# Keys one step ahead, row norms in groups, the second tile's load on another queue, cached latents loaded sooner

## The chip, the cores and the metric

The kernel runs on one core of a Trainium2 chip. The metric is device time in microseconds (us) of one execution; of a set of runs the median counts. In the profile TensorE is PE (matmuls) and PEld (its weight loads), VectorE is DVE, ScalarE is ACT, GpSimd is POOL and SyncE, which issues the transfers, is SP. Each engine works through its own queue in order and waits on semaphores for what other engines and transfers make.

## What is computed

Two layers of a streaming encoder with three kinds of heads side by side, for 1024 prompt frames (8 tiles of 128) and 32 sample frames (a ninth tile), 1024 wide. A layer is, cut to what matters here:

```python
h = _rmsnorm(x, norm_g)                      # x * rsqrt(mean(x*x) + EPS) * g
z = h @ w_in                                 # retention | latent attention | chunk band
ret_o = retention(...)                       # 4 heads, decayed state
cq, ckv_new, kr_new = ...                    # low-rank queries, latent keys and values, shared rope key
ckv_all = concat(past ckv, ckv_new)          # the sample's 128 cached latents come first
kv = ckv_all @ mla_w_ukv;  q = cq @ mla_w_uq # 8 heads, keys of 64 + 32
mla_o = softmax(q k / sqrt(96)) v            # chunk-causal in the prompt, dense in the sample
band_o = softmax(q k / 8 + bias) v           # the last 8 chunks of 64
y = x + concat(ret_o * silu(g_a), mla_o * silu(g_b), band_o * silu(g_c)) @ w_out
```

All of it is float32; matrix products are made of a high and a low part of each operand.

## The kernel before

**Stages.** For each layer `layer_in` (line 1447) multiplies the nine tiles by eleven column blocks of `w_in`, in the order of STEPS (line 42): b (the latents) first, then blocks for retention and the band, and four blocks of gates. `chunk` (line 525) does a block for eight of them: for each of the nine tiles eight row groups of three matmuls into a bank of tag pj (two banks), then a callback that unloads the bank. `mla` (line 823) then walks over 64 units (head pair, block of 128 queries, head) of scores, transposes and values, while the output product `out_part` (line 1398) is put between the units.

**The order of the work.** Everything beside the main loops is a generator in a list of tasks (`spawn`, line 253). After each step of a main loop `poll` (line 298) advances those tasks that are ready by a hand-made clock (a task is ready again 450 ns after its last step unless GAPS says otherwise), that don't exceed the number allowed for their kind (STREAMS: three prep tasks, two b tasks, one mla task at a time) and that have pages: all tiles in SBUF come from 60 pages of 512 columns (`page`, `free`), and `safe` (line 256) keeps enough of them for the tasks that have started. That is the program's order. The framework then orders each engine's instructions by a timeline model of its own (line 1660), with the program's order as priority; tasks of kind mla have a raised one (line 51).

**The opening.** For the first layer the tiles come transposed from memory. `first_prep` (line 482) is a task per tile: it loads two halves xt, all on SP; splits them into high and low parts in the arena H; squares and sums them (ScalarE, GpSimd, and a reduction xsq on VectorE); has a matmul with ones sum over the partitions, copies that sum (st, line 503) and makes the row's norm r from it on GpSimd (`rstd`). The rows' norms are applied after the projection: as a scale where a bank is unloaded (`unload`, line 551, for which r is enough), and in the gates, where rows lie along the columns, by a product with rb. For that the task spreads r over 128 columns (rrep, line 509), transposes it on TensorE and copies it into rb. `run` (line 1542) starts the opening by hand:

```python
self.step_task(self.fg[0])      # loads of tile 0
self.fetch(0, "b", E0)          # eight weight tiles of block b
self.step_task(self.fg[0])      # parts of tile 0
self.step_task(self.fg[1])      # loads of tile 1
self.poll()
```

When tile 2 of block b is done, `load_bias` (line 393) builds the band's bias: rows are copied to memory (bt), read back with a step (braw), and made into bT on VectorE.

**The sample's cached latents.** `cache_task` (line 611) takes the 128 cached latents through the same products as a tile: it loads cc (two transfers), transposes it on TensorE at once, and goes on with `kv_task`. It is spawned at the ninth tile of block b and runs when two b tasks or fewer are before it.

**The keys.** `mla_pair` (line 786) turns the keys and queries of two heads into transposed high and low parts in H. It has four turns (keys and queries, two halves each); a turn's two loads (sk or sq, from the buffers kd and qd in memory) are issued in the step of the turn before, but those of the first turn in the same step as its transposes. The first pair of a layer is a task that starts in the last gate block and has to be finished before the units begin; the other three are advanced by `mla` one step per unit, from the third of the 16 units of a head pair on.

Of the kernel before, what the change touches and what calls it, by code (L numbers as in the profile page):

```python
# [13 lines left out]
OP = mybir.AluOpType  # L14
# [6 lines left out]
NS = 32  # L21
# [77 lines left out]
class Kern:  # L99
# [382 lines left out]
    def first_prep(self, t, hT):  # L482

        A = self.A
        n = 128 if t < 8 else NS
        xt = [self.page([4, n], name="xt") for _ in range(2)]
        for j in range(2):
            self.load(xt[j], (A["xt_p"][t] if t < 8 else A["xt_s"])[:, 4 * j:4 * j + 4])
        yield
        for j in range(2):  # L490
            self.parts(t, j, xt[j], hT, LO0[j])
        yield
        for x in xt:
            self.act(x, x, AF.Square, scale=1.0 / 32)
        self.tt(xt[0], xt[0], xt[1], OP.add, eng="G")
        sq = self.page([n], name="xsq")
        self.red(sq, xt[0].rearrange("p k n -> p n k"))
        self.free(*xt)
        yield
        p = self.bank((1,), "prep")  # L500
        self.mm(p[:n], sq, self.ones, True, True)
        s1 = self.st(1)
        self.nc.vector.tensor_copy(s1[:n], p[:n])
        r = self.rstd(s1, n, 1, self.r0[:, t:t + 1])
        self.free(sq)
        self.prepped.add(t)
        yield
        rep = self.page([128], name="rrep")
        self.ts(rep[:n], r[:n].to_broadcast([n, 128]), 1.0, None, OP.mult)
        p = self.bank((n,), "prep")  # L510
        self.tr(p, rep[:n])
        self.free(rep)
        self.act(self.rb[t // 4][:, 128 * (t % 4):128 * (t % 4) + n], p)
        yield

    def new_hT(self):
        self.prepped = set()
# [92 lines left out]

    def cache_task(self, l):
        A = self.A
        c = self.page([160], name="cc")
        self.load(c[:, :128], A["c_ckv"][l, 0])
        self.load(c[:, 128:160], A["c_kr"][l, 0])
        p = self.bank((128,), "b")
        self.tr(p, c[:, :128])
        ch, cl = self.page([3, 128], F32R, name="cch"), self.page([3, 128], F32R, name="ccl")
        self.hilo(p, ch[:, 2], cl[:, 2])
        yield  # L620
        yield from self.kv_task(l, 9, 128, ch, cl, c[:, 128:160])
        self.free(c, ch, cl)
        self.b_done()
# [162 lines left out]
    def mla_pair(self, l, hp):  # L786

        turns = [(name, half) for name in ("k", "q") for half in range(2)]
        src = dict(k=self.kd[l], q=self.qd[l])

        def stage(name, half):
            r = []
            for b in (2 * half, 2 * half + 1):
                t = self.page([2, 192], name="s" + name)
                self.load(t, src[name][hp, 256 * b:256 * b + 256, :].rearrange("(a p) e -> p a e", p=128))
                r.append(t)
            return r

        nxt = stage(*turns[0])
        self.vals[hp] = []  # L800
        for n, (name, half) in enumerate(turns):
            cur = nxt
            if n < 3:
                nxt = stage(*turns[n + 1])
            j, col = (0, 1) if name == "k" else (2, 0)
            for i in range(2):
                hs = self.sets[(2 * hp + i) % 4]
                p = self.bank((4, 128), "mprep")
                for b in range(4):
                    self.tr(p[:96, b], cur[b // 2][:, b % 2, 96 * i:96 * i + 96])  # L810
                pf = p[:96].rearrange("p a b -> p (a b)")
                sl = slice(512 * half, 512 * half + 512)
                self.hilo_g(pf, self.cols[:96, col:col + 1], hs[:96, j, sl], hs[:96, j + 1, sl])
                if i:
                    self.free(*cur)
                if n == 3 and not i:
                    for b in range(2):
                        t = self.page([4, 128], name="sv")
                        self.load(t, self.vd[l][hp, 512 * b:512 * b + 512, :].rearrange("(a p) e -> p a e", p=128))
                        self.vals[hp].append(t)  # L820
                yield
# [625 lines left out]
    def layer_in(self, l, hT):  # L1447
        A = self.A
        w = A["w_in"][l]
        self.qs, self.ks, self.vs = [None] * 2, [[None] * 2 for _ in range(2)], [None] * 2  # L1450
        self.mix, self.mixed = {}, set()
        self.bks = None
        self.spare = False
        self.turns, self.full, self.bfull, self.scored = 0, 0, 0, False
        self.bk, self.bv, self.bqt, self.bvp, self.buse = {}, {}, {}, {}, {}
        self.bleft = NB + 2
        self.bq, self.bkdone = set(), set()
        zk = {}

        def cb_b(t, p):  # L1460
            self.spawn("b", self.b_task(l, t, self.unload(t, p, 416)), lambda: "u" in self.W)
            if t == MISC_T:
                self.spawn("misc", self.misc_task(l))
            if t == 8:
                self.spawn("b", self.cache_task(l), lambda: "u" in self.W)
                self.spawn("smp", self.mla_sample(l), lambda: not self.bleft)

        def cb_ak(t, p):
            zk[t] = self.page([512], name="zk")
            self.unload(t, p, 256, z=zk[t][:, :256])  # L1470

        def cb_av(t, p):
            self.unload(t, p, 256, z=zk[t][:, 256:])

        def cb_aq(t, p):
            if t == 0:
                self.ret_state(l)
            self.spawn("ret", self.ret_task(l, t, zk.pop(t), self.unload(t, p, 256)))

        def cb_ck(t, p):  # L1480
            self.spawn("bk", self.band_k_task(l, t, self.unload(t, p, 256)))

        def cb_cv(t, p):
            self.band_v(l, t, p)

        def cb_cq(t, p):
            self.spawn("bq", self.band_task(l, t, self.unload(t, p, 256)))
            if t < 8 and t % 2 == 1:
                pr = t // 2
                self.spawn("band", self.band_attn(l, pr), lambda: all(  # L1490
                    x in self.bq and x in self.bkdone for x in (2 * pr, 2 * pr + 1)) and (not pr or pr - 1 in self.buse))

        fts = dict(ag=(0, 1), bg0=(2, 3), bg1=(4, 5), cg=(6, 7))
        cbs = dict(b=cb_b, ak=cb_ak, av=cb_av, aq=cb_aq, ck=cb_ck, cv=cb_cv, cq=cb_cq)

        def gen(name):
            if name in fts:
                return self.gates(self.W.pop(name), fts[name], hT, name == STEPS[-1])
            return self.chunk(self.W.pop(name), 416 if name == "b" else 256, hT, cbs[name])

        self.spawn("mla", self.mla_pair(l, 0), lambda: self.turns >= 4 and not self.bleft)
        for name, nxt in zip(STEPS, STEPS[1:] + (None,)):
            todo = ([("u", AHEAD_U)] if name == "b" else []) + ([(nxt, AHEAD)] if nxt else [])
            if name not in self.W:
                self.press(lambda: not self.safe(NEED_W[name]))
                self.fetch(l, name)
            n = 0
            for _ in gen(name):
                n += 1
                if todo and n >= todo[0][1] and self.safe(NEED_W.get(todo[0][0], 9)):  # L1510
                    self.fetch(l, todo.pop(0)[0])
                self.poll()
                self.press(lambda: len(self.fg) > CAP or not self.safe(2))
            for x, _ in todo:
                self.press(lambda: not self.safe(NEED_W.get(x, 9)))
                self.fetch(l, x)
# [25 lines left out]
    def run(self):  # L1542
        A = self.A
# [7 lines left out]
        rows = lambda y: (lambda t: y[128 * t:min(T, 128 * t + 128)])  # L1551
        for t in range(9):
            self.spawn("prep", self.first_prep(t, hT))
        self.step_task(self.fg[0])
        self.fetch(0, "b", E0)
        self.step_task(self.fg[0])
        self.step_task(self.fg[1])
        self.poll()
        self.load(self.tab, A["tab"])
        self.load_layer(0)  # L1560
# [1 line left out]
        for l in range(DEPTH):  # L1562
# [22 lines left out]
            bulk, need, n = [None, None], [0, 0], 0.0  # L1585
# [10 lines left out]
            for x, _ in enumerate(self.mla(l)):  # L1596
# [5 lines left out]
                n = min(n + RATES[2 if ended[0] else x % 16 >= SMALL], 2.0)  # L1602
                while n >= 1:
                    i = int(ended[0])
# [62 lines left out]
```

## Time and profile before

| | |
|---|---|
| median of 3 runs | 1388.73 us (1382.41, 1388.73, 1390.26) |
| the profiled execution | 1391.21 us |
| its span, first to last instruction | 1389.4 us |
| mean granted clock of TensorE | 0.992 |
| instructions | 28577 |
| ScalarE, VectorE, GpSimd busy | 760.1, 849.3, 463.7 us |
| transfers | 130.56 MB, 94 GB/s over the span |

The profile is of one execution, with times from the start of its span. A wait names the engine and line that waited, then what it waited for. A line in the code can be that of a helper (177 is every matmul, 183 every transpose, 187 every ScalarE operation), so tiles tell more than lines. PEclk is the share of full clock that TensorE was granted: 1.00 is 2.4 GHz and 0.50 is 1.2 GHz.

### The profile page before, as it was taken

The numbers are of one execution on the slowest core, as the hardware profiler recorded it, in microseconds if no ns is written. First come the engines' busy times: TensorE is split into PE (matmuls) and PEld (weight loads), VectorE is DVE, ScalarE is ACT, GpSimd is POOL, SyncE is SP. The second block draws the span as 40 slices with busy tenths as digits, with TensorE's granted clock in tenths as the row PEclk, the third lists the DMA queues.
The fourth block names the chain that finished last, engine by engine and source line by source line (L and its number), as shares of the span: only waits on it lengthen the run. The fifth ranks groups of instructions, "written<-read, shape, count | busy, mean of one in ns | idle before, by whom it ended". The sixth has DMA issues, their size and how long they took to land.

```text
span 1389.4 us, 28577 instructions
## 1 busy us (share of the span) xinstructions
PE 1327.5 (96%) x10339; PEld 1213.8 (87%) x10339; DVE 849.3 (61%) x2564; ACT 760.1 (55%) x2186; POOL 463.7 (33%) x686
## 2 busy tenths in 40 slices
PE   6899999999998899999999999999999999999998
PEld 6899989999898788877889999989989988888787
DVE  7655657666766656665562555655766765666543
ACT  6545545353655756676672445454555665766551
POOL 4655767343000312221123456755420012312110
PEclk9999999999999999999999999999999999999999
DMA  7334341131211433522340344221212123433131
GB/s 237 106 91 148 116 115 39 39 92 36 64 51 34 145 109 109 159 72 89 107 154 12 110 130 136 82 68 32 85 43 76 47 81 118 148 111 115 61 127 65
DMA packets 131077, 130.56 MB, mean 94 GB/s; under 512 B 14392, under 2 KB 107256, under 8 KB 130936
## 3 DMA queue, kind: packets, MB, share of 16 engines
q1 hardware_dynamic: 130936, 128.74, 30.0%
q8 instruction: 81, 1.33, 0.4%
q14 instruction: 60, 0.49, 0.1%
HBM read 84.48 MB, written 45.79 MB: 94 GB/s over the span
## 4 chain that ended last, share of the span: by engine, by line
PE 76%; DMA 9%; DVE 5%; ACT 4%; POOL 2%; issue 2%; SPq 1%; ACTq 0%; DVEq 0%; POOLq 0%
PE pj L177 46%; PE ps L177 10%; PE s L177 10%; PE ps L183 7%; DMA raw<-in_w_in 3%; PE pj L183 2%; DMA sk<-kd 2%; POOL rs L242 2%; DMA raw<-in_w_out 1%; PE s L183 1%; SPq L247 1%; DMA braw<-bt 1%; ACT whi L187 1%; DVE st L214 1%; ACT PT L187 1%
## 5 line engine op out<-in xcount | busy, mean ns | idle before, releaser
L177 PE MATMUL pj<-whi,H 128*128 128x256 f32 (+1 forms) x1792 | 368.1, 297 | 12.8 <-DVE whi L203 7.1
L177 PEld LDWEIGHTS pj<-whi,H 128*128 128x128 f32 x1792 | 295.1, 192 | 16.8 <-ACT xt L187 7.0
L177 PE MATMUL pj<-wlo,H 128*128 128x256 f32 (+1 forms) x896 | 264.8, 296 | 1.3 <-DVE wlo L210 1.3
L177 PE MATMUL pj<-H,whi 128*128 128x256 f32 (+1 forms) x1024 | 205.6, 293 | 4.0 <-DVE th L210 1.6
L195 POOL TENSOR_TENSOR mlo<-mix,mhi 128x256 fp32r<-128x256 f32 x96 | 70.1, 750 | 378.7 <-ACT mhi L187 179.0
L187 ACT ACTIVATE PT<-ps 128x384 f32<-128x384 f32 (+3 forms) x304 | 130.9, 456 | 113.4 <-PE ps L183 112.4
L177 PEld LDWEIGHTS pj<-wlo,H 128*128 128x128 f32 x896 | 171.9, 192 | 3.6 <-DVE wlo L210 2.2
L177 PEld LDWEIGHTS pj<-H,whi 128*128 128x128 f32 x1024 | 163.0, 191 | 7.3 <-DVE th L210 2.0
L242 POOL TENSOR_TENSOR rs<-ms,nhalf 128x4 f32<-128x4 f32 (+5 forms) x141 | 165.1, 1171 | 9.2
L177 PE MATMUL pj<-H,wlo 128*128 128x256 f32 (+1 forms) x512 | 149.2, 291 | 0.3 <-DVE wlo L210 0.3
L203 POOL TENSOR_SCALAR ms<-st 128x4 f32<-128x4 f32 (+6 forms) x166 | 59.3, 357 | 229.3 <-DVE st L214 194.6
L177 PE MATMUL s<-H 96*128 96x384 f32 (+3 forms) x516 | 128.9, 364 | 3.1 <-ACT P L187 2.9
L187 ACT ACTIVATE whi<-raw,cols 128x256 fp32r<-128x256 f32 (+2 forms) x178 | 83.2, 516 | 75.8 <-DMA raw<-in_w_in 59.7
L214 DVE TENSOR_REDUCE st<-s 128x1 f32<-128x384 f32 (+3 forms) x220 | 118.3, 538 | 8.9 <-PE s L177 6.6
L210 DVE SCALAR_TENSOR_TENSOR wlo<-raw,cols,whi 128x256 fp32r<-128x256 f32 (+2 forms) x184 | 90.7, 525 | 47.7 <-ACT whi L187 47.0
L187 ACT ACTIVATE P<-s,st 128x384 f32<-128x384 f32 (+3 forms) x172 | 99.9, 588 | 22.3 <-DVE st L203 21.9
L177 PE MATMUL pj<-whi,mhi 128*128 128x512 f32 x256 | 103.2, 403 | 3.5 <-DVE st L203 2.2
L177 PE MATMUL pj<-wlo,mhi 128*128 128x512 f32 x256 | 100.7, 393 | 0.0
L177 PE MATMUL pj<-whi,mlo 128*128 128x512 f32 x256 | 100.5, 396 | 0.1
L177 PEld LDWEIGHTS pj<-H,wlo 128*128 128x128 f32 x512 | 98.0, 191 | 1.4 <-DVE wlo L210 0.9
L195 POOL TENSOR_TENSOR wlo<-raw,whi 128x512 fp32r<-128x512 f32 x32 | 40.7, 1285 | 169.5 <-PE s L177 113.5
L177 PEld LDWEIGHTS s<-H 96*128 96x128 f32 x516 | 84.0, 189 | 12.8 <-ACT P L187 6.1
(262 smaller groups left out, 2816.0 us busy)
## 6 DMA issues: line engine op xcount, KB each, us to landing
raw<-in_w_in SPq DMA_DIRECT2D x80, 256.0 KB, 3.1
raw<-in_w_out SPq DMA_DIRECT2D x32, 256.0 KB, 2.9
yp<-yres SPq DMA_DIRECT2D x32, 256.0 KB, 2.0
yres<-yp SPq DMA_DIRECT2D x32, 256.0 KB, 2.8
qd<-qn SPq DMA_DIRECT2D x32, 192.0 KB, 1.9
kd<-kt SPq DMA_DIRECT2D x32, 192.0 KB, 2.0
sk<-kd SPq DMA_DIRECT2D x32, 192.0 KB, 3.6
sq<-qd SPq DMA_DIRECT2D x32, 192.0 KB, 2.6
```

The lines of the kernel that those rows point to most:

```text
L177: self.nc.tensor.matmul(out, lhsT, rhs, start=start, stop=stop)
L183: self.nc.tensor.transpose(out, in_, self.ident[:k, :k])
L187: r = self.nc.scalar.activation(out, in_, func, **kw)
L195: (self.nc.vector if eng == "D" else self.nc.gpsimd).tensor_tensor(out, a, b, op=op)
L203: (self.nc.vector if eng == "D" else self.nc.gpsimd).tensor_scalar(out, a, s1, s2, op0=op0, **kw)
L210: self.nc.vector.scalar_tensor_tensor(out, a, s, b, op0=op0, op1=op1)
L214: self.nc.vector.tensor_reduce(out, in_, axis=AX.X, op=op, negate=negate)
L242: self.nc.gpsimd.tensor_tensor(r[:n], ms[:n], self.nhalf[:n, :w], op=OP.pow)
L247: self.nc.sync.dma_start(dst, src)
```

## The change

Four edits. A `yield` in `mla_pair` makes a step of its own of the first turn's loads. `first_prep` ends at the norm r, and a new task `row_norms` spreads the norms of four tiles at a time into rb; it is spawned at the ninth tile of block b in the first layer. The second tile's loads are issued by ScalarE and stand, with tile 0's, ahead of the fetch of the weights. The cached latents are loaded in the callback of the eighth tile of block b (t == 7), into a page that is held until `cache_task` ends.

```diff
@@ -485,7 +485,8 @@
         n = 128 if t < 8 else NS
         xt = [self.page([4, n], name="xt") for _ in range(2)]
         for j in range(2):
-            self.load(xt[j], (A["xt_p"][t] if t < 8 else A["xt_s"])[:, 4 * j:4 * j + 4])
+            (self.nc.scalar if t == 1 else self.nc.sync).dma_start(
+                xt[j], (A["xt_p"][t] if t < 8 else A["xt_s"])[:, 4 * j:4 * j + 4])
         yield
         for j in range(2):
             self.parts(t, j, xt[j], hT, LO0[j])
@@ -501,17 +502,24 @@
         self.mm(p[:n], sq, self.ones, True, True)
         s1 = self.st(1)
         self.nc.vector.tensor_copy(s1[:n], p[:n])
-        r = self.rstd(s1, n, 1, self.r0[:, t:t + 1])
+        self.rstd(s1, n, 1, self.r0[:, t:t + 1])
         self.free(sq)
         self.prepped.add(t)
         yield
-        rep = self.page([128], name="rrep")
-        self.ts(rep[:n], r[:n].to_broadcast([n, 128]), 1.0, None, OP.mult)
-        p = self.bank((n,), "prep")
-        self.tr(p, rep[:n])
-        self.free(rep)
-        self.act(self.rb[t // 4][:, 128 * (t % 4):128 * (t % 4) + n], p)
-        yield
+
+    def row_norms(self):
+
+        for g, n in enumerate((128, 128, NS)):
+            m = 4 if g < 2 else 1
+            rep = self.page([m, 128], name="rrep")
+            self.ts(rep[:n], self.r0[:n, 4 * g:4 * g + m].unsqueeze(2).to_broadcast([n, m, 128]), 1.0, None, OP.mult)
+            yield
+            p = self.bank((m, n), "prep")
+            for i in range(m):
+                self.tr(p[:, i], rep[:n, i])
+            self.free(rep)
+            self.act(self.rb[g], p.rearrange("p a b -> p (a b)"))
+            yield
 
     def new_hT(self):
         self.prepped = set()
@@ -610,9 +618,7 @@
 
     def cache_task(self, l):
         A = self.A
-        c = self.page([160], name="cc")
-        self.load(c[:, :128], A["c_ckv"][l, 0])
-        self.load(c[:, 128:160], A["c_kr"][l, 0])
+        c = self.cc
         p = self.bank((128,), "b")
         self.tr(p, c[:, :128])
         ch, cl = self.page([3, 128], F32R, name="cch"), self.page([3, 128], F32R, name="ccl")
@@ -797,6 +803,7 @@
             return r
 
         nxt = stage(*turns[0])
+        yield
         self.vals[hp] = []
         for n, (name, half) in enumerate(turns):
             cur = nxt
@@ -1461,7 +1468,13 @@
             self.spawn("b", self.b_task(l, t, self.unload(t, p, 416)), lambda: "u" in self.W)
             if t == MISC_T:
                 self.spawn("misc", self.misc_task(l))
+            if t == 7:
+                self.cc = self.page([160], name="cc")
+                self.load(self.cc[:, :128], A["c_ckv"][l, 0])
+                self.load(self.cc[:, 128:160], A["c_kr"][l, 0])
             if t == 8:
+                if self.rb is not None:
+                    self.spawn("prep", self.row_norms())
                 self.spawn("b", self.cache_task(l), lambda: "u" in self.W)
                 self.spawn("smp", self.mla_sample(l), lambda: not self.bleft)
 
@@ -1551,10 +1564,12 @@
         rows = lambda y: (lambda t: y[128 * t:min(T, 128 * t + 128)])
         for t in range(9):
             self.spawn("prep", self.first_prep(t, hT))
-        self.step_task(self.fg[0])
+        first, second = self.fg[:2]
+        self.step_task(first)
+        self.step_task(second)
         self.fetch(0, "b", E0)
-        self.step_task(self.fg[0])
-        self.step_task(self.fg[1])
+        self.step_task(first)
+        self.step_task(second)
         self.poll()
         self.load(self.tab, A["tab"])
         self.load_layer(0)
```

## Rows read from the trace of the kernel before

**Rows 1.** The page, part 1: busy us (share of the span) and instructions

```profile
PE 1327.5 (96%) x10339; PEld 1213.8 (87%) x10339; DVE 849.3 (61%) x2564; ACT 760.1 (55%) x2186; POOL 463.7 (33%) x686
```

**Rows 2.** PE's waits, whole span: line, releaser, us in total, times, longest

```profile
PE pj L183 <- DMA sk<-kd: 4.9, 5, 1.2
PE s L183 <- DVE rrep L203: 4.7, 1, 4.7
...
PE s L177 <- DVE xsq L214: 2.3, 1, 2.3
...
PE ps L183 <- DMA cc<-in_c_ckv: 2.2, 1, 2.2
```

**Rows 3.** Stretches of the opening: us, engines' busy us, PEclk, DMA share, GB/s

```profile
7.00:15.50 8.50, 7.17 (x19) 5.99 (x20) 8.50 (x15) 4.42 (x7) 1.30 (x1) 1.00 1.01 361
...
38.50:43.30 4.80, 0.07 (x2) 0.03 (x2) 1.37 (x5) 1.26 (x7) 1.17 (x3) 0.96 0.58 177
43.30:50.00 6.70, 6.70 (x22) 6.45 (x23) 5.28 (x18) 5.49 (x13) 5.12 (x11) 0.52 0.51 153
```

**Rows 4.** DVE's timeline, 41 to 46 us: start, us, instruction [idle before]

```profile
41.66 0.62 DVE L203 TENSOR_SCALAR bT<-braw 128x256 f32<-128x256 f32 x2 [4.17 <-DMA braw<-bt]
...
43.00 0.22 DVE L203 TENSOR_SCALAR rrep<-r 128x128 f32<-128x128 f32 x1
...
44.99 0.14 DVE L503 COPY st<-s 128x1 f32<-128x1 f32 x1
```

**Rows 5.** POOL's and ACT's timelines, 47 to 49 us

```profile
47.80 0.80 POOL L242 TENSOR_TENSOR r<-ms,nhalf 128x1 f32<-128x1 f32 x1
...
48.63 0.61 ACT L187 ACTIVATE z<-pj,r 128x416 f32<-128x416 f32 x1
```

**Rows 6.** Chain of waits, 0 to 80 us: start us, us, what

```profile
24.30 4.63 PE pj L177 x24
...
44.40 7.10 PE pj L177 x24
```

**Rows 7.** Tiles rrep and rb: operation, count, min/median/max ns, first and last start us

```profile
L203 DVE TENSOR_SCALAR rrep<-r x9: 213/227/1312, 19.9 to 67.2; 128x128 f32<-128x128 f32 x8, 32x128 f32<-32x128 f32 x1
...
L187 ACT ACTIVATE rb<-s x9: 228/269/297, 24.0 to 70.0; 128x128 f32<-128x128 f32 x8, 128x32 f32<-128x32 f32 x1
...
L195 DVE TENSOR_TENSOR u<-pj,rb x40: 180/424/426, 243.0 to 441.9; 128x256 f32<-128x256 f32 x32, 128x32 f32<-128x32 f32 x8
```

**Rows 8.** SP's and POOL's timelines at the opening

```profile
2.58 3.75 SPq L247 DMA_DIRECT2D raw<-in_w_in  x8
6.48 2.07 SPq L247 DMA_DIRECT2D xt<-in_xt_p  x4
...
19.85 2.52 POOL L195 TENSOR_TENSOR xt<-xt,xt 128x512 f32<-128x512 f32 x2
```

**Rows 9.** Transfers, whole span: count, KB each, median us to landing

```profile
xt<-in_xt_p SPq DMA_DIRECT2D x16, 256.0 KB, 4.9
```

**Rows 10.** PE's timeline, 410 to 415 and at 915 us

```profile
410.02 0.42 PE L183 MATMUL pj<-ident,sk 128*96 128x128 f32 x2 [1.14 <-DMA sk<-kd]
...
414.67 0.60 PE L183 MATMUL pj<-ident,sk 128*96 128x128 f32 x4
...
915.20 0.33 PE L183 MATMUL ps<-ident,cc 128*128 128x128 f32 x1 [2.15 <-DMA cc<-in_c_ckv]
```

**Rows 11.** Stretches at the band attention and the cached latents (columns as rows 3)

```profile
421.80:428.60 6.80, 6.39 (x48) 5.74 (x49) 2.02 (x10) 1.16 (x4) 0.00 (x0) 0.50 0.44 130
428.60:470.00 41.40, 36.28 (x344) 33.21 (x344) 27.57 (x110) 27.84 (x88) 5.88 (x6) 1.00 0.22 65
...
916.70:920.10 3.40, 3.40 (x16) 3.27 (x16) 2.10 (x8) 2.49 (x7) 2.00 (x2) 0.50 0.00 0
```

**Rows 12.** Chain of waits, whole span: two steps 16 units apart

```profile
511.85 3.97 DMA sk<-kd
...
566.56 4.00 DMA sk<-kd
```

## The prediction

> **What bounds the kernel now.** I read four views in this order. First the page's busy times: TensorE (PE) is busy for 1327.5 of 1389.4 us [rows 1], so the other engines cost time only where they make PE stop, and all its stops together are 1389.4 - 1327.5 = 61.9 us. Second, the waits of PE: four of the things it waits for are touched by the change [rows 2], the loads of the keys (sk, 4.9 us in 5 stops), the spread row norm (rrep, 4.7 us in one), the squared sums (xsq, 2.3 us in one) and the sample's cached latents (cc, 2.2 us in one). That is 14.1 us, a fifth of the idle time. Third, the stretches with PE's granted clock, because a stop is followed by slow work: after the rrep stop PE is busy throughout 43.3 to 50 us, at a clock of 0.52 [rows 3], and 1.5 us after the cc stop it runs 3.4 us at 0.50 [rows 11]. Fourth, the timelines at each stop, to see what the missing input itself waited for.
>
> The sum is made against the profiled execution (1391.2 us, span 1389.4). It stands 2.5 us above the median of the three runs, 1388.7, so a total found on it is taken off the median.
>
> **Part 1, row norms in groups.** The nine rrep copies on VectorE (DVE), of about 0.23 us, and nine evacuations into rb on ScalarE, of about 0.27 us [rows 7], become three and three; the nine transposes on PE stay. All move from the opening to after the last tile of the first projection. They are first read at 243 us [rows 7], some 170 us later, so the moved work lies beside PE's projection work and I cost it at nothing; without that cover three groups would stop PE for at most a DVE operation each, about 1 us in all.
> What counts is where the old rrep stood. At 38.5 us PE meets a transpose of rrep. DVE can't make it: its queue stands before bT, which waits 4.17 us for the band bias's rows (braw), and rrep comes behind bT, at 43.00 [rows 4]. So PE does nothing from 38.5 to 43.3 (0.07 us busy of 4.80) [rows 3]. The 24 matmuls of the next tile were ready, and then run at the half clock: 7.10 us, against 4.63 us for 24 at full clock [rows 6]. The stop costs 4.73 and the clock 2.47, together 7.2 us.
> Not all of it comes back. DVE still waits for braw. Behind bT stands also the copy st at 44.99 [rows 4], from which GpSimd makes the norm r at 47.80, which ScalarE needs for the unload z at 48.63 [rows 5]; only that frees one of the two banks of tag pj, which the tile after next needs. PE would then work on its ready tile from 38.5 to about 43.2 and stop again until 48.63 + 0.61 = 49.2, where before it began that later tile at about 52.1: 2.9 us gained. That is the low end; 7.2 is the high end, if the copy st now comes ahead of bT, as its matmul, no longer behind the transpose, runs 5 us earlier. I take 5.0, the middle.
>
> **Part 2, the second tile's load on ScalarE.** Two loads of 256 KB [rows 9] leave ScalarE's queue ahead of the eight weight loads, where SyncE (SP) had issued them at 6.48, behind those (2.58 to 6.33) [rows 8]. Issuing costs ScalarE nothing: it has no tile to work on before the first one has landed. The gain is the xsq stop of 2.3 us [rows 2]: GpSimd's sum for that tile came at 19.85 [rows 8], and an earlier tile lets it come earlier. The price: the transfer engines are full here (share 1.01 at 361 GB/s) [rows 3], so 512 KB put ahead of the weights delay them by up to 512 KB / 361 GB/s = 1.45 us, and the first matmul with them. The lower bound is 0: a weight tile serves three matmuls, at half clock 7.10 / 8 = 0.9 us [rows 6], so the weights behind the first have time. I take the middle, 0.7. Net -1.6 us, between +1.45 and -2.3.
> A rule of the Trainium skill speaks against this part: "Trainium Kernel Development and Optimization", section Key Constraints, says that loads issued from several engines' queues all run on the same 16 transfer engines and interleave, so that another queue saves only time of issue. By it the sum would take the whole 1.45 us, leave part 2 at -0.85 and end at 1380. No load leaves another queue than SP's in this trace, so it doesn't show this.
>
> **Part 3, the cached latents.** In each layer two small loads move from the start of the cache task (912 us in layer 1) to the eighth tile of the first projection, over 100 us earlier; on SP that is the same issues in another place, behind nothing but their page. Layer 0 doesn't stop PE for them. In layer 1 the transpose waits 2.15 us [rows 10], and the half clock from 916.7 takes half of 3.40 us, 1.7 [rows 11]. High end 3.9; low end 0, if PE then waits for something else. I take 3.0, the whole stop and half of the clock. The cost is one page of 60 held through the layer's projections. With 59 left I put it at nothing; were a fetch of weights to wait for it, PE would stop about as it does here, for 2.2 to 3.9 us a time.
>
> **Part 4, the keys a step ahead.** The first two loads of a head pair are issued one step before their transposes: per layer four pairs, the same 32 loads in all. In the attention stage a step is one unit, (566.56 - 511.85) / 16 = 3.4 us [rows 12], while the loads of a step take 4.0 us [rows 12] and the five stops are about 1 us each, 1.2 at most [rows 2], the one at 410.02 among them [rows 10]. A load 3.4 us earlier covers each of them. High end 4.9 us, all of [rows 2]'s sk line; low end 0. I take 3.5, since behind some stops PE next waits for a DVE result of the scores. The pair's work then ends one step later of sixteen, which its readers, a whole head pair further on, don't see; the first pair of a layer is the exception (third rival).
>
> **Sum:** 5.0 + 1.6 + 3.0 + 3.5 = 13.1 us. Program order changes on every queue from the first microseconds on, so small stops elsewhere (48 of the 61.9 us are not touched) are drawn anew; I take off 3 us, as a removed stop seldom leaves all later ones as they were. That leaves 10: 1388.7 - 10 = **1379 us**.
>
> **The rivals.** (a) The DVE queue decides the opening: it still stands 4.17 us at bT, and the stop only moves from the transpose to the pj bank. For it: the st to z chain [rows 4, 5]. Against: the copy's matmul is ready 5 us sooner. Then part 1 gives 2.9 less a new half-clock stretch of 2.5, so 0.4; total 0.4 + 1.6 + 3.0 + 3.5 - 3 = 5.5, or 1383 us, no change that can be told.
> (b) The change doesn't do what it says on the queues: the issue order is made by a scheduler from a timeline model, and a load that is earlier in the program may stay where it was. For it: nothing forces SP to issue sk before the step; against: the loads so far left when their step came, or PE would not have had to wait for them. Part 4 gives nothing, and the total is 10 - 3.5 = 6.5, or 1382 us, just within.
> (c) Slower: the first pair's extra step. Each layer starts its attention only once that pair is done, in a stretch in which PE has little else: from 428.6 to 470 it is busy for 36.28 of 41.40 us, and from 421.8 to 428.6 at clock 0.50 [rows 11]. The first two steps of the pair lie 414.67 - 410.02 = 4.65 us apart [rows 10]. A step more costs up to 4.65 plus a half-clock stretch of 3.4 in each of two layers, 16.1 us, and is felt where the projections' work ends before the pair does. If also part 1 gives only its 0.4, the total is 16.1 - 0.4 - 1.6 - 3.0 - 3.5 + 3 = +10.6, or 1399 us. Against it: the extra step adds no work, and the scores of the chunk band stand beside it.
>
> **How the numbers follow.** A measurement can tell about 0.5%, 6.9 us, from no change: faster is below 1381.8, slower above 1395.6. Forecast 0.51 and, with all terms at their high ends, 0.06, both faster; (a) 0.18 and (b) 0.15, both within; (c) 0.10, slower. So faster 0.57, same 0.33, slower 0.10. The low end of the range takes all high ends, 7.2 + 2.3 + 3.9 + 4.9 = 18.3, and half the spread of the three runs, 4 us: 1366. The high end takes (a) with (b), 1388.7 - 2, and the same 4 us with a little of (c): 1392. The cases of "faster" alone hold 1366 to 1382.
>
> **What would show it.** In the changed profile: no rrep row among PE's waits and no long PE stop at 38.5; the stretch that held 43.3 to 50 at clock 0.9 or more; no cc and no sk in PE's waits; the second tile's loads on ScalarE's queue within 3 us, and the first matmul at 7.1 to 8.5; PE idle of 50 to 54 us in all instead of 61.9. I am wrong in part 1 if PE stops 4 us or more between 38 and 50 us for H or for a pj bank; in part 4 if sk waits stay; in the whole if PE's idle time outside the four lines grows by more than 5 us, in the stretch of (c) above all.

## The result and the profile after

The changed kernel takes 1409.12 us, median of 4 runs (1407.32 to 1410.15), beside 1387.3 us for the kernel before on the same chip (4 runs): 1.0161 times as long, 95% interval 1.0141 to 1.0181. I had forecast 1379, and 1366 to 1392 as the range; it is 22 us slower. The profiled execution took 1410.15 us, its span is 1407.6 us, its mean granted clock 0.984.

First the busy times of the changed kernel, from part 1 of the profile's page, to be read against [rows 1]:

```profile
span 1407.6 us, 28566 instructions
...
PE 1340.1 (95%) x10339; PEld 1220.5 (87%) x10339; DVE 846.5 (60%) x2556; ACT 762.0 (54%) x2178; POOL 458.1 (33%) x686
```

The same 10339 matmuls keep PE busy for 12.6 us more, and PE's stops come to 1407.6 - 1340.1 = 67.5 us, 5.6 more. Next PE's waits in the changed kernel (line, releaser, us in total, times, longest), the counterpart of [rows 2]:

```profile
PE pj L177 <- DVE whi L203: 8.1, 1, 8.1
PE pj L177 <- ACT zk L187: 7.8, 3, 3.2
PE s L177 <- ACT P L187: 5.9, 7, 1.7
PE ps L183 <- ACT P L187: 4.6, 8, 1.4
PE s L177 <- DVE xsq L214: 3.9, 1, 3.9
...
PE pj L183 <- DMA sk<-kd: 0.7, 2, 0.5
```

The four lines that the change aimed at fell from 14.1 us to 4.6: no rrep and no cc are left, sk fell from 4.9 to 0.7, and xsq rose from 2.3 to 3.9. Other waits grew by more than that: the first matmul begins at 8.1 us instead of 7.1, and a bank of tag pj that ScalarE unloads into zk is waited for 7.8 us instead of 3.7.

The longer busy time is half-clock time. These are the stretches between the opening's start and the last microseconds at which the granted clock was at its lower level (1.2 GHz), first of the kernel before, then of the changed one (us, busy us and count of each engine, PEclk, DMA share, GB/s; the last line sums them):

```profile
42.90:49.70 6.80, 6.42 (x21) 6.18 (x22) 5.61 (x20) 5.49 (x13) 4.82 (x10) 0.50 0.56 169
...
sum 20.40, PE 19.62 PEld 18.49 DVE 12.55 ACT 11.21 POOL 6.82; mean PE 4.90 PEld 4.62 DVE 3.14 ACT 2.80 POOL 1.71
```

```profile
110.90:114.30 3.40, 3.40 (x18) 3.40 (x17) 1.58 (x4) 1.43 (x8) 1.93 (x3) 0.50 0.54 175
...
1029.10:1039.30 10.20, 10.20 (x48) 7.88 (x48) 4.42 (x16) 4.31 (x14) 1.25 (x2) 0.50 0.13 32
...
sum 44.20, PE 41.70 PEld 36.93 DVE 24.82 ACT 26.97 POOL 16.33; mean PE 5.21 PEld 4.62 DVE 3.10 ACT 3.37 POOL 2.04
```

Four stretches have become eight. In the changed kernel's opening one 128x416 matmul follows another after 0.35 us in the half-clock stretch from 26 us on, and after 0.19 us at 15 to 16 us, at full clock. Full clock would thus have saved about 45% of PE's time in such stretches: by that estimate 0.45 x (41.7 - 19.6) = 10 of the 12.6 us come from there. So beside the kernel before, the loss is small stops, spread over both layers, and half-clock work behind some of them. Where the old rrep stop was, the clock did get better, though not to the 0.9 that I had named: 43.3 to 50 us now has 0.75 instead of 0.52 [rows 3]. The stretch at 916.7 to 920.1, behind the old cc stop, has 1.00 instead of 0.50 [rows 11].

### The profile page after: what moved, and what is told of

Same layout as the page of the kernel before. It is cut to its first block, busy times and chain, and to the rows that moved or that the text cites. A ratio compares the mean times of both kernels' runs of the same rounds, so it can differ in the third digit from the quotient of the medians.

```text
span 1407.6 us, 28566 instructions
## 1 busy us (share of the span) xinstructions
PE 1340.1 (95%) x10339; PEld 1220.5 (87%) x10339; DVE 846.5 (60%) x2556; ACT 762.0 (54%) x2178; POOL 458.1 (33%) x686
## 5 line engine op out<-in xcount | busy, mean ns | idle before, releaser
L177 PE MATMUL pj<-H,whi 128*128 128x256 f32 (+1 forms) x1024 | 209.4, 295 | 4.6 <-DVE th L210 2.6
L242 POOL TENSOR_TENSOR rs<-ms,nhalf 128x4 f32<-128x4 f32 (+4 forms) x141 | 166.1, 1178 | 9.5
L203 POOL TENSOR_SCALAR ms<-st 128x4 f32<-128x4 f32 (+5 forms) x166 | 55.5, 334 | 241.1 <-DVE st L214 194.8
```

The costliest lines, as they stand in the source:

```text
L177: self.nc.tensor.matmul(out, lhsT, rhs, start=start, stop=stop)
L203: (self.nc.vector if eng == "D" else self.nc.gpsimd).tensor_scalar(out, a, s1, s2, op0=op0, **kw)
L242: self.nc.gpsimd.tensor_tensor(r[:n], ms[:n], self.nhalf[:n, :w], op=OP.pow)
```

## The experiments

Theories: **(P)** the page that part 3 holds from the eighth tile of block b until the cache task ends is short elsewhere, and what goes without it comes late; **(R)** any edit draws the order of all queues anew, and this draw came out badly; **(T)** part 3's transfers themselves, or part 2's, collide with weights. All ratios are to the kernel before, run on the same chip beside it. Letters name the parts: r row norms, a second tile, c cached latents, y keys a step ahead.

**Each part alone,** put into the kernel before; the full lines stand in the diff above. s1 (a):

```diff
-            self.load(xt[j], ...)
+            (self.nc.scalar if t == 1 else self.nc.sync).dma_start(xt[j], ...)
@@ run
-        self.step_task(self.fg[0])
+        first, second = self.fg[:2]
+        self.step_task(first)
+        self.step_task(second)
         self.fetch(0, "b", E0)
...
```

s2 (r) takes the spread out of `first_prep`, s3 (c) loads and holds early, s4 (y) adds the step:

```diff
+                if self.rb is not None:                      # s2, at t == 8
+                    self.spawn("prep", self.row_norms())
```

```diff
+            if t == 7:                                       # s3
+                self.cc = self.page([160], name="cc")
+                self.load(self.cc[:, :128], A["c_ckv"][l, 0])
+                self.load(self.cc[:, 128:160], A["c_kr"][l, 0])
```

```diff
         nxt = stage(*turns[0])
+        yield                                                # s4
```

> The kernel before with one of the four edits: the second tile's loads issued by ScalarE ahead of the weights. Three theories of where the +22 us come from. Spread: every edit redraws the order of work, the loss is many small stops in places that no edit touches, and the four single edits give between -6 and +8 us each and don't add up to +22. Held page: the cached latents' page, held from the eighth tile on, is nearly all of the loss; this edit without it gives -4 to +2 us, 1383 to 1389. Pair's step: the extra step of a head pair makes the loss; here again -4 to +2. The changed kernel's own opening (the first matmul 1.1 us later, the stop for xsq 3.9 us instead of 2.3) should be seen here if it is this edit's: a first matmul at 8.1 us.

> The kernel before with the row norms spread in groups after the first projection, and nothing else. My forecast of its part: the stop of 4.7 us for rrep goes, -3 to -7 us, 1380 to 1384. Spread: -6 to +8 us. Held page and pair's step: -5 to 0, since neither is here. If the 9 us that the changed kernel loses between 75 and 120 us come from the spreading now being done there, this kernel loses them too and stands at 1390 or more.

> The kernel before with the cached latents loaded at the eighth tile into a page that is held until their task, and nothing else. Held page: +10 to +22 us, 1397 to 1409, with waits of ScalarE for stores (a page that is written again before its store has landed) and PE stops behind them between 70 and 400 us in layer 0. Spread: -6 to +8. Pair's step: -4 to 0, as the cc stop of 2.2 us goes.

> The kernel before with the first pair of key loads in a step of its own, and nothing else. Pair's step: +9 to +22 us, most of it in layer 1's attention (1040 to 1340 us in the changed kernel, which loses 14 us there). Held page: -5 to 0, the sk stops of 4.9 us gone. Spread: -6 to +8 us.

Measured: a 1.0052 (1.0033 to 1.0070), +7 us; r 0.9967 (0.9945 to 0.9989), -4.6 us by the ratio, -2.9 by the medians; c 1.0069 (1.0046 to 1.0093), +9.6 us; y 0.9985 (0.9963 to 1.0006), -2.1 us. Two parts gain a little, two lose; together they make +10, give or take some 6 by their intervals, so about 12 of the 22 us appear only when they are combined.

**What of part 3 costs.** s5 issues the transfers as early in the program and holds no page:

```diff
+        self.cc = cp.tile([128, 160], F32, name="cc")     # in setup
@@ cb_b
+            if t == 7:
+                self.load(self.cc[:, :128], A["c_ckv"][l, 0])
+                self.load(self.cc[:, 128:160], A["c_kr"][l, 0])
```

s6 is the change without part 3 (r, a and y). s7 is r and y with the tile of s5. s8 is the kernel before with fewer pages:

```diff
-N_PAGES = 60
+N_PAGES = 59
```

> The kernel before with the two transfers of the cached latents issued at tile 7, as in the change, but into a constant tile of their own (640 bytes a partition), so that no page is held for them. If the held page is what the third part costs, this loses what that part lost alone (399.02 - 388.04 = +11 us over the kernel before) and keeps its gain, the 2.15 us wait and the slow clock after it: 2 to 4 us under the kernel before, about 1385. If instead the earlier transfers themselves collide with weights on their way in, it is as slow as the third part alone, about 1399. If any new plan costs some us by chance, it lies anywhere from 1384 to 1394.

> The changed kernel with its third part taken out: cached latents loaded in their own task, as before. The three parts that stay, each alone, came to +7.3, -2.9 and -1.8 us, sum +2.6. If the held page carries the loss, this is 1409 - 11 or lower, 1391 at the sum. If the parts cost more together than alone, wherever they are combined, it stays above 1400.

> Row norms in groups, keys a step ahead and the latents early into a tile of their own; the second tile stays on SyncE's queue and no page is held. If the second tile's transfer and the held page are the two parts that lose, this one gains what is left: -2.9 - 1.8 - 3 = about -8, 1380, and between 1376 and 1384. If combining re-plans loses by itself, it is no better than the kernel before, 1386 or more.

> The kernel before with 59 pages for the whole run in place of 60; nothing else is edited. If a page is worth what the third part alone lost, this is slower than the kernel before by about as much or more, since the page is gone everywhere and not only from tile 7 to the cache task: 1396 to 1410. If the price of the held page was only another order drawn by chance, it lies within 5 us of 1388, on either side. My forecast put one page of 60 at nothing.

Measured: s5 1.0050 (1.0032 to 1.0069, 5 runs); s6 1.0008 (0.9995 to 1.0021); s7 0.9990 (0.9970 to 1.0011); s8 1.0443 (1.0411 to 1.0476), 1445.93 us. So part 3 costs all of the 22 us in the change that can be told (1409 against 1387), and one page of 60 is worth 60 us to a kernel that is otherwise unedited, where I had put it at nothing. s5 is a miss: with no page held it still lost 7 us, and its interval overlaps that of s3, which holds the page. So alone in the kernel before, the page's price can't be told from what s5 pays without it. In s7 the same tile and transfers cost nothing that can be told. Nor is s5 a test of the change's own transfers (T): its tile waits for no page, and the scheduler moved the loads. These are the loads of cc in s5, and in s9 (below), where a page holds them (count, min/median/max ns, first and last start us):

```profile
L247 SPq DMA_DIRECT2D cc<-in_c_ckv x2: 352/395/438, 23.0 to 207.7; - x2
```

```profile
L247 SPq DMA_DIRECT2D cc<-in_c_ckv x2: 340/348/357, 61.9 to 725.4; - x2
```

In the change they start at 62.0 and 735.0 us, in s5 at 23.0, among the opening's loads, and at 207.7, still in layer 0; s7 (28.4 us) and s12 (26.4) have moved them likewise. Why s5 loses 7 us stays open.

In the changed kernel PE falls behind between 54 and 130 us; this is the stretch in the changed kernel, in s6 and in s8 (columns as above):

```profile
54.00:130.00 76.00, 70.16 (x484) 67.39 (x483) 35.28 (x119) 35.17 (x111) 41.75 (x70) 0.98 0.29 86
```

```profile
54.00:130.00 76.00, 76.00 (x560) 73.98 (x559) 39.28 (x126) 38.66 (x120) 42.94 (x69) 1.00 0.34 105
```

```profile
54.00:130.00 76.00, 66.56 (x458) 63.30 (x457) 36.08 (x116) 33.78 (x108) 40.82 (x71) 0.96 0.27 82
```

Without part 3 PE never stops there and does 560 matmuls; with it 484; with 59 pages 458. SP's timeline of the same stretch shows that the weights come late (start us, us, what), first in the changed kernel, then in s6:

```profile
61.98 0.38 SPq L247 DMA_DIRECT2D cc<-in_c_ckv  x1
62.40 0.46 SPq L247 DMA_DIRECT2D cc<-in_c_kr  x1
63.78 9.71 SPq L250 DMA_DIRECT2D qd<-qn  x3
...
85.55 0.39 SPq L247 DMA_DIRECT2D raw<-in_w_in  x1
```

```profile
75.09 0.38 SPq L247 DMA_DIRECT2D raw<-in_w_in  x1
...
77.53 0.37 SPq L247 DMA_DIRECT2D raw<-in_w_in  x1
...
82.01 0.37 SPq L247 DMA_DIRECT2D raw<-in_w_in  x1
...
83.47 0.46 SPq L247 DMA_DIRECT2D raw<-in_w_in  x1
```

After the loads that both issue by 43 us, s6 fetches its next four weight tiles at 75 to 84 us; the changed kernel fetches the first of them at 85.55. The latents' loads start at 62 us, and their page stays taken until the cache task, whose transpose starts at 202 us, 140 us later, and in layer 1 187 us later. This is the tile cc in the changed kernel (operation, count, min/median/max ns, first and last start us):

```profile
L247 SPq DMA_DIRECT2D cc<-in_c_ckv x2: 372/374/376, 62.0 to 735.0; - x2
...
L183 PE MATMUL ps<-ident,cc x2: 270/271/272, 202.6 to 922.1; 128*128 128x128 f32 x2
```

The pages that are left are also wanted again before their last store has landed. These are ScalarE's waits for stores in the changed kernel from 54 to 130 us, 8.5 us; in s6 there is one, of 1.8 us:

```profile
ACT sq L187 <- DMA kd<-kt: 3.6, 2, 1.8
...
ACT z L187 <- DMA bd<-z: 2.0, 1, 2.0
ACT vp L187 <- DMA qd<-qn: 1.5, 1, 1.5
...
ACT zk L187 <- DMA vd<-vp: 1.4, 1, 1.4
```

The longest stop in the zk line among PE's waits, 3.23 us up to 78.35 us, ends with an unload of a pj bank that itself waited 1.45 us for such a store:

```profile
77.82 0.47 ACT L187 ACTIVATE zk<-pj,r 128x256 f32<-128x256 f32 x1 [1.45 <-DMA vd<-vp]
```

The cause on the builder's side can be counted: at each moment of its own clock, does `safe` refuse pages to some kind of work? That clock is the hand-made one of the program, not a time on the chip; a count is of moments and kinds of work.

```
pages refused at     50-100   850-900   whole run
before                  1        11        192
s3  (c)                29        15        211
the change             30        14        206
s6  (r, a, y)           0        11        180
s8  (59 pages)         27         3        286
s9  (change, 61)        0         0        134
s11 (r, y)              0        11        182
s16 (latents a step)    0        41        216
s17 (s16, 61)           0         8        181
```

In the change the refusals begin at 54.5, the moment at which the page is taken, and last up to 66.5. Half of the 30 are the main loop's, which goes on only while `safe(2)` grants it two pages; the other half are steps of b tasks. With the same two b tasks under way, s6 has 7 free pages at 54.5 and goes on, the change has 6 and is refused: one page is the whole difference. So the main loop stands before its last step of block b until 69.3, where s6 makes that step at 57.3. No fetch of weights is refused there. The next one hangs on the count of the main loop's steps, and comes at 89.1 instead of 76.9; that is the late weights in SP's timeline.

**A page more.** s9 is the change, s10 the kernel before, with 61 pages; s11 is r and y; s12 is the change with the tile of s5 in place of the page:

```diff
-N_PAGES = 60
+N_PAGES = 61
-        self.sp = ec(tc.tile_pool(name="stats", bufs=32))
+        self.sp = ec(tc.tile_pool(name="stats", bufs=30))
-        t = self.sp.tile([128, 16], F32, tag="st", name=self.nm(name))
+        t = self.sp.tile([128, 8], F32, tag="st", name=self.nm(name))
```

> The changed kernel, whole, with 61 pages in place of 60; the room for it comes from the small statistics tiles, 30 of 8 words a partition in place of 32 of 16. If the page that stays held from tile 7 on is what the change loses by, the 61st gives it back: 1387, as the change without its third part, or under it. If the loss is the early transfers themselves, or a plan that came out badly by chance, it stays near 1409 (above 1400).

> The kernel before with 61 pages and the same small statistics tiles, otherwise unedited: the other side of the run with 59, which took 1446, 60 us more. If each page is worth tens of microseconds here, this gains some 10 to 30 us. If 60 is where the pages stop being short, it is within 5 us of the kernel before. If any new plan costs by chance, it may be slower by some microseconds.

> Row norms in groups and keys a step ahead, nothing else. Alone they came to -2.9 and -1.8 us beside 20 to 28 runs of the kernel before. If they add, -4 to -6: 1380 to 1383. If two re-plans together lose by chance what each gains, 1386 or more. Beside it stands the run that also had the latents early in a tile of their own: 1384.35, 1.3 us under its kernel before, so that this one tells what those transfers cost.

> The changed kernel, whole, except that the cached latents are loaded at tile 7 into a constant tile of their own and not into a page. If the loss is in the held page, this falls from 1409 to what the change has without its third part, 1387, give or take the 5 us that the own tile alone showed. If the loss is in the early transfers as they stand in this plan, it stays above 1400.

Measured: s9 0.9987 (0.9967 to 1.0007), 1387.49 us; s10 1.0015 (0.9995 to 1.0035); s11 0.9996 (0.9978 to 1.0014); s12 1.0018 (0.9995 to 1.0042). One page more gives the change all of its 22 us back, with nothing else of it undone, and so does the tile of its own. The loads of s9 start where the change's do (61.9 and 725.4 us), so as they stand there they cost nothing that can be told: for the change (T) falls. To the kernel before the 61st page is worth nothing. So its 60 are just enough: the next one down costs 60 us, the next one up gains none. The stretch of 54 to 130 us in s9 is that of s6 again:

```profile
54.00:130.00 76.00, 76.00 (x559) 73.99 (x558) 39.22 (x125) 38.51 (x120) 42.80 (x69) 1.00 0.35 106
```

This is its busy line:

```profile
PE 1333.0 (96%) x10339; PEld 1216.2 (88%) x10339; DVE 845.7 (61%) x2557; ACT 761.4 (55%) x2181; POOL 461.5 (33%) x686
```

Its span is 1384.4 us, so PE's stops come to 51.4. Beside s9, its nearest twin, the changed kernel has 16 us more of stops and 7 more of busy time: stops are the larger part of what the missing page costs. s9, level with the kernel before, has itself seven half-clock stretches ahead of its last microseconds, 30.8 us in all.

This speaks for (P). Against (R): s6, s7, s9, s10, s11 and s12 are six other draws, all within 0.2% of the kernel before. A draw can cost something, as s5 shows, but none without the held page came near 22 us. s11 is a miss too: r and y alone made -4.6 and -2.1, together 0.

**Where part 2's loss comes from, and a shorter hold.** s13 has only the first hunk of s1, ScalarE's queue; s14 only its second, the new order in `run`; s15 is a with r; s16 is r and y with one step between the latents' load and their transpose:

```diff
         self.load(c[:, 128:160], A["c_kr"][l, 0])
+        yield
         p = self.bank((128,), "b")
```

> Of the second part only the queue: ScalarE issues the second tile's two loads, but the opening's steps stay in the order of before (weights first in the program). Both halves of the part together cost 7.3 us. If the cost is that 512 KB go ahead of the weights on shared transfer engines, this costs as much, since ScalarE's queue is free from the start and its loads start as early: about 1395. If it is the opening's order (tile 1 split before the first weights on VectorE), this is at the kernel before, 1386 to 1390.

> Of the second part only the order: the second tile's loads stay on SyncE, but stand ahead of the fetch of the weights. By the shared transfer engines they then delay the weights as the change's do, and SyncE issues the eight weight loads behind four loads and not two: 1395 or a little more. If the other queue is what costs, about 1388.

> Second tile's load (alone +7.3 us) and row norms in groups (alone -2.9 us), nothing else. If they add, +4: 1392. If the second tile's cost is a longer stop for the spread row norm (6.47 us in its own run, against 4.73, 1.59 and 3.94 in three runs with the row norms as before), it goes with the norms: 1384 to 1388.

> Row norms in groups, keys a step ahead, and the cached latents loaded one step of their own task before their transpose, so that the page is held for a step more and not for 116 us of the plan (145 in layer 1). If the time for which the page is held is what costs, this keeps the gain of the earlier load without the price: 2 to 4 us under the same kernel without it, so 1384 to 1387 where that one stood at 1389.47 beside 1389.43. If any earlier load of the latents costs, as the one into a tile of its own did (+7), it is slower than the kernel before by 3 us or more.

Measured: s13 1.0029 (1.0015 to 1.0044); s14 1.0017 (0.9997 to 1.0036); s15 1.0001 (0.9986 to 1.0016); s16 1.0194 (1.0167 to 1.0221), 1416.55 us. The queue alone costs 4.0 us; the order alone 2.4 by the ratio, 0.6 by the medians, with an interval that reaches no change. The first matmul begins at 8.2 us in s13, at 8.5 in s1 and at 9.8 in s14, against 7.1. In s14 SP issues the weights from 3.53 us on instead of 2.58, behind two more loads. Beside the row norms part 2 costs 4.7 us (s15 against s2), beside r and y 1.7 (s6 against s11), which is within the noise of those two runs. In the profiled execution of s1 the rrep stop was 6.5 us long, one line of its PE waits:

```profile
PE s L183 <- DVE rrep L203: 6.5, 1, 6.5
```

so a part of what a costs alone may go with that stop, but not all; as the stop's length varies between executions (last section), this isn't shown.

s16 was the largest miss: I had expected the price to go with the time for which the page is held, and one step of hold lost 27 us against s11. The count above says where. s16 takes its page at the same moments as s11, 185.2 and 840.7 of the builder's clock, but goes on to the transpose only at 191.0 and 846.2, where s11 does so at once. The second time pages are short behind it: from 850 to 900 the refusals rise from 11 to 41, and the main loop stands at one step from 854.0 to 873.4, which s11 passes from 850.8 to 852.6. On the chip PE loses ground there; this is 905 to 1045 us in s11 and in s16:

```profile
905.00:1045.00 140.00, 136.48 (x1226) 128.07 (x1225) 95.53 (x311) 72.10 (x223) 59.45 (x81) 0.99 0.19 54
```

```profile
905.00:1045.00 140.00, 128.45 (x1077) 119.23 (x1077) 77.37 (x245) 58.48 (x171) 58.52 (x85) 0.94 0.18 51
```

**Page or order of steps, and which layer.** s17 is s16 with 61 pages (the edits of s9). s18 is the change with part 3 in layer 1 alone:

```diff
-            if t == 7:
+            if t == 7 and l == 1:
```

> The kernel of the last run (norms, pair, latents one step of their task before their transpose: 1416.55, 27 us more than the same without that step) with 61 pages in place of 60. If that step lost because one page was held over it at a moment when none could be spared, the 61st page gives it back: 1387 to 1392, where the other kernels with 61 pages stand. If it lost because the task's later steps come a turn later, whatever the pages, it stays above 1405.

> The changed kernel with the early load and the held page in layer 1 alone; in layer 0, where no stop stood for the latents, they are loaded in their task as before. Against the changed kernel without its third part the changed one is 13 us behind at its 1200th matmul (205 us), 9 at the 2700th (382 us), 8 at the 7500th (1018 us) and 23 near the end. If each layer pays for its own held page, 9 us of the 22 come back: 1400. If the loss sits in layer 0 alone, it is 1387; if in layer 1 alone, 1409.

Measured: s17 1.0022 (1.0001 to 1.0043), 1393.03 us; s18 1.0079 (1.0049 to 1.0108), 1400.34 us. s18 came out as (P) has it, and s17 in the main, 1 us above the range that I had named: the same steps with one page more lose 3 us and not 27, with 1244 matmuls in the stretch where s16 had 1077:

```profile
905.00:1045.00 140.00, 139.27 (x1244) 129.87 (x1243) 88.78 (x291) 68.18 (x208) 57.06 (x80) 0.99 0.18 52
```

And each layer pays for its own held page: 9 us by the medians, 11 by the ratios, come back when layer 0 is left out. The count of refusals shows layer 0's price plainly; layer 1's, spread over 905 to 1300 us, shows in it hardly at all (14 against 11), so there the link rests on s9, s12 and s18. How the page makes layer 1's loss is not shown: in the profiled executions the change is 8 us behind s6 at the 7500th matmul (1018 us) and 23 near the end, and the latents' transpose is at 922.1 us.

## Why the prediction was wrong, point by point

**The step that failed** is in part 3: "The cost is one page of 60 held through the layer's projections. With 59 left I put it at nothing". In the change it cost 22 us (s6 against the changed kernel), and the same size came back by a 61st page (s9) or a tile apart (s12). The branch that I named beside it, a fetch of weights that waits for the page, came near. The fetch was late by 10 us on SP's queue (85.55 for 75.09), but it was not refused itself: the main loop was, and the fetch behind it came late. I priced that branch at 2.2 to 3.9 us a time, left it out of the sum and out of the range, and made no rival of it, though it was the one cost of the change that lasts (140 and 187 us of hold). What was missing was a count of the free pages at the moment at which the page is taken. The program has it: in the kernel before the free pages fall to 4 between 50 and 100 of its clock, in a stretch in which two b tasks run that are reckoned to need 10 each (NEED). "59 left" counted the pages there are, not the free ones.

**Part 3's gain** (3.0): the cc stop is gone, as forecast, with the slow clock behind it. But s7 against s11 (0.9990, 0.9996) and s12 against s6 (1.0018, 1.0008) show no gain that can be told from an early load even without the page, though its loads stood elsewhere; in s7 a stop for ccl, 1.05 us, follows in its place. The term was at its low end, 0, as far as these runs can tell.

**Part 2** (1.6 us gained) had the wrong sign: +7 alone, +1.7 to +4.7 in company. The price at the first matmul, +1.1 to +1.4 us, is near the 1.45 of my upper bound. By the rule of the Trainium skill that I weighed ("Trainium Kernel Development and Optimization", section Key Constraints: several queues share the transfer engines, another queue saves time of issue only) that was to be expected, and the trace agrees: ScalarE's queue lets the first matmul begin at 8.2 to 8.5 us where SP's has it at 9.8, but neither at 7.1. (With that rule the prediction's own terms end at 1379.4, not at the 1380 that stands there.) The gain I had set against it did not come. The second tile's sum is indeed made at 14.5 us instead of 22.8, but PE now stops at the same place, for 3.87 us, for the third tile's; these are DVE's xsq in the changed kernel and the matmul that waited for it:

```profile
14.52 1.06 DVE L214 TENSOR_REDUCE xsq<-xt 128x128 f32<-128x512 f32 x1
...
24.20 1.02 DVE L214 TENSOR_REDUCE xsq<-xt 128x128 f32<-128x512 f32 x1 [1.16 <-POOL xt L195]
```

```profile
25.28 0.38 PE L177 MATMUL s<-ones,xsq 128*128 128x1 f32 x2 [3.87 <-DVE xsq L214]
```

**Part 1** (5.0 between 2.9 and 7.2): right in mechanism, 2.9 to 4.6 alone. In s2 PE is busy throughout 38 to 50 us, with no stop for a pj bank; in the whole change another stop came there, 2.95 us for DVE's bn at 44.55. One reason for the lower value is that the rrep stop of the profiled execution, 4.73 us, was a long one: in s4, whose PE instructions stand in the same order up to the first head pair, it was 1.6 us (last section).

**Part 4** (3.5): right in mechanism, -2.1 alone; sk fell to 0.7 us in the change, but in s4 only to 2.9, in two stops, so a load one step earlier did not cover each stop. The loads did move on SP's queue: in s4 the first pair's start 6.1 us before their transposes (403.29 and 409.43 us) instead of 4.2, so rival (b) falls. Rival (c) falls as well: s4, which has the extra step alone, is not slower.

**The sum and its 3 us of scatter.** Without part 3 I would have had 5.0 + 1.6 + 3.5 - 3 = 7 us faster; s6 measured +1. Part 2 explains some of it; that r and y together gave nothing (s11) stays open. Several runs were to show that the parts add, and none did. I had said that I would be wrong "in the whole if PE's idle time outside the four lines grows by more than 5 us"; it grew from 47.8 to 62.9 us, and half-clock work came on top, which my sum had charged only to stops that go and not to stops that come (rivals (a) and (c) had one such stretch each).

No version beats the kernel before by more than r alone, 0.9967 (0.9945 to 0.9989); the whole change with 61 pages is level with it.

## What to carry to other kernels

Where tiles come from a fixed pool, an edit that holds one for longer is priced by the free tiles at that moment and by who is refused, not by the size of the pool: take one tile away and add one, and the two times tell at once whether the pool binds (here +60 and 0 us). An early load into such a pool needs a tile to spare. And a stop that is removed is worth what it is on the average of executions, not what one trace shows.

## What was not expected of the hardware

The length of one stop varies between executions with the same order of work: the stop for rrep was 4.7 us in the kernel before, 1.6 in s4 and 2.4 in s3, although every queue of the three has the same instructions in the same order up to 55 us. The transpose behind it starts at 42.6 to 43.3 us in all three; PE came to it later in s4, after 6.8 us at a granted clock of 0.50 from 23.7 us on, where the kernel before ran at 1.00. The stop ahead of that stretch was the same in both, 2.3 us for xsq: slow work followed it in one and not in the other. And the two ways to load the second tile early differ by nearly the transfer's length (1.45 us by the prediction's estimate): 8.5 us to the first matmul by ScalarE's queue (s1), 9.8 by SP's (s14), for the same 512 KB ahead of the same weights. Of these 1.3 us, SP's later start on the weights (3.53 us instead of 2.61 in s1) makes 0.9; the rest is within the spread of that first matmul over the kernels here with ScalarE's queue, 8.1 to 8.6 us.
